# Down projection of a diffusion step: block sums of the activations formed in the gated unit, sums of the gate weights kept in scratch

## The chip, the cores and the metric

The kernel runs on one core of one Trainium2 chip. The metric is the device time of one launch in microseconds (us). PE is TensorE (PEld its weight loads), DVE VectorE, ACT ScalarE, POOL GpSimd and SP SyncE, on whose queue all transfers between DRAM and SBUF are issued, in order.

## The reference

One layer of a hybrid diffusion model is applied to 256 context tokens and 2048 latent tokens of 1024 features, in float32: modulated norm, an input projection, a gated DeltaNet scan beside a chunked mixer, an output projection with residual. Then comes the part that the change touches, the feed-forward block with D_FF = 2816, and a final norm:

```python
def swiglu(h, w_gate, w_up, w_down):
    return (jax.nn.silu(h @ w_gate) * (h @ w_up)) @ w_down

    h = rmsnorm(x, norm2_g) * (1 + sc2) + sh2
    x = x + g2 * swiglu(h, w_gate, w_up, w_down)
```

## The kernel before

The kernel is generated by a Python program with a small model of the engines (Model, line 44). Side work is written as generators, which a list of tasks (spawn, tick) inserts between matmuls at times that this model gives; a store is held in a list and issued (flush) when the model thinks that its source is ready, or when its source's buffer is to be reused. So the program's order on every engine follows from the model. lighter(n) picks VectorE or GpSimd for an elementwise operation by the model. The helper at line 149 issues every operation, so all rows of the profile carry that line and are told apart by their tiles.

Every matmul of the feed-forward block is split in three, since its operands are held as a rounded high part and a low part (split_to: a cast on ScalarE, then a subtraction on VectorE): high x high, low x high, high x low.

**The gated unit.** The 18 tiles of 128 tokens are handled in three groups (gi) of six, paired as three pairs. Within a group a loop runs over 22 column blocks f of w_gate and w_up (128 columns each), one unit each. Gate and up weights of one block, each cut into two halves of the 1024 rows, form a 2 x 2 block matrix (a11, a12 from w_gate, a21, a22 from w_up), and two token tiles form the other (b11, b12, b21, b22). Their product is formed with seven block products instead of eight (Winograd's form of Strassen's scheme), j = 0 to 6, with these left blocks:

- a11; s2 = s1 - a11; s3 = a11 - a21; a12; s1 = a21 + a22; a22; s4 = a12 - s2

One product j is 12 matmuls of 128 x 384 into one of six PSUM banks (pm), so a unit is 84. After each product, one or two additions on VectorE gather the results (tiles s, u, up); silu runs on ScalarE. The two results of a unit, gate times up for the first and for the second tile of each pair, go to DRAM scratch (fa_d, named a).

Loading and splitting of weights: w_load(i) loads both weight blocks of unit i (two of 512 KB) into tiles fraw, two units ahead. w_prep(i, j) forms the sums s1 to s4 (four per unit, in all 66 units, on VectorE or GpSimd) and splits block j of unit i into the tile wu, one unit ahead of its use. The right blocks of a group lie in seven tiles hb0 to hb6 (h2). For the groups 1 and 2 they are made while the group before runs (stage_next: normalise, transpose, split into tiles hu, store to scratch fh_d, named hbd), and loaded when the last unit of that group has used the tile (hb<-hbd). The last unit of group 0 or 1 isn't begun until stage_next has been issued completely.

In group 2 down_sums reads w_down (tiles dx), forms the four weight sums of the second block product (tiles do) and stores them (fw_d, named wt). The last unit of group 2 isn't begun until it has been issued completely.

**The down projection.** Now the activations are the left matrix, with two token tiles and two halves of D_FF (11 blocks f each) as blocks 11, 12, 21, 22, and w_down with its halves the right one. The nine pairs are handled in two runs of five and four. A run has seven products q, and in each a slot for every pair: 63 slots of 33 matmuls of 128 x 512 (11 blocks k, three parts). The product of slot s needs one left block of 704 KB, split into the tile ah. a_load(s) loads what it is made of into four buffers ar: three blocks for q = 0, two for q = 1, 2 and 5, one for q = 3, 4 and 6. a_prep(s) forms the sum of q = 1, 2 and 5 on VectorE (s1 for later slots is formed at q = 0, and s1 and s2 are stored in scratch fs_d, named sp), and splits. At the start of slot s, a_prep(s + 1) and a_load(s + 2) are issued. Right blocks are loaded into ur and split into un, one product ahead (u_load, u_step). From q = 3 on, every slot completes a quarter of two tiles' output (piece: times the gate g2b, on VectorE or GpSimd, plus the residual, square sum on ScalarE); finish normalises a tile's row block and stores it.

second_first prepares the first slots during the last unit of group 2.

Of the kernel before, what the change touches and what calls it, by code (L numbers as in the profile page):

```python
# [16 lines left out]
KB = 8  # L17
# [143 lines left out]
def hybrid_step(  # L161
# [375 lines left out]
    with tc.manual_schedule():  # L537
# [1233 lines left out]
        NW = 10  # L1771
        order_a = []
        groups = [[], [], []]
        fst = {}
        fa_d = [[dram.tile([P, HN, NFF, P], F32, name=f"a{gi}{i}") for i in range(2)] for gi in range(3)]
        fh_d = [[dram.tile([P, 2, 4, HN, P], F32, name=f"hbd{gi}{j}") for j in range(7)] for gi in range(3)]
        fw_d = [dram.tile([P, 4, 512], F32, name=f"wt{k}") for k in range(HF)]
        fs_d = [[dram.tile([P, HF, P], F32, name=f"sp{i}{p}") for p in range(NT // 2)] for i in range(2)]

        def f_open():  # L1780
# [7 lines left out]
            w_load(0)  # L1788
            spawn(w_first())

        def w_first():
            yield list(wraw[0])
            for j in range(7):
                w_prep(0, j)
                yield ()
            w_load(1)
# [5 lines left out]
        wraw, wtmp, wu = {}, {}, {}  # L1802

        def w_load(i):
            if i < 3 * NFF:
                f = i % NFF
                wraw[i] = [W.tile([P, KB, P], F32, tag="hh" if i > 1 else "fraw", name="fraw", bufs=NB if i > 1 else 2)
                           for _ in range(2)]
                for r, w in zip(wraw[i], (w_gate, w_up)):
                    nc.sync.dma_start(r, w[:, f * P:(f + 1) * P].rearrange("(k p) c -> p k c", p=P))  # L1810

        def w_prep(i, j):

            if i >= 3 * NFF:
                return
            F1 = fst["F1"]
            rg, ru = wraw[i]
            a11, a12, a21, a22 = rg[:, 0:4], rg[:, 4:8], ru[:, 0:4], ru[:, 4:8]
            if j == 0:
                wtmp[i] = [F1.tile([P, 4, P], F32, tag="wt", name=f"ws{n}", bufs=3) for n in (1, 2)]  # L1820
                lighter(512).tensor_add(wtmp[i][0], a21, a22)
            s1, s2 = wtmp[i]
            if j == 1:
                lighter(512).tensor_sub(s2, s1, a11)
            elif j == 2:
                lighter(512).tensor_sub(a21, a11, a21)
            elif j == 6:
                lighter(512).tensor_sub(s2, a12, s2)
            x = (a11, s2, a21, a12, s1, a22, s2)[j]
            u = F1.tile([P, 2, 4, P], F32R, tag="wu", name="wu", bufs=NW)  # L1830
            split_to(u[:, 0], u[:, 1], x)
            wu[i, j] = u
            if j == 6:
                del wraw[i], wtmp[i]
# [479 lines left out]
```

## Time and profile before

| | us |
|---|---|
| three runs | 3299.15, 3297.8, 3293.04 (median 3297.8) |
| profiled execution | 3295.81 |
| its span | 3294.1 |
| first and last matmul start of the gated unit | 1610.7 and 2667.6 |
| first and last matmul start of the down projection | 2698.9 and 3284.0 |
| busy in the span: PE, DVE, ACT, POOL | 2985.2, 2248.0, 1377.8, 699.9 |
| mean granted TensorE clock | 0.955 |

The profile gives, for one execution, busy times and waits. In a row of the timeline stand start, duration, engine, operation, out<-in by the names of tiles, shape and count, and in brackets the idle time before it with what ended it (the releaser). Rows of a tile give smallest, median and largest duration in ns, then first and last start. Rows of waits give who waited, for what, the sum in us, how often and the longest. In windows, a row is one stretch of the span in us from its start. Matmuls overlap, so their durations are longer than their pace. DMA share is the mean busy share of the core's 16 DMA engines.

### The profile page before, as it was taken

What the parts mean: (1) busy time and instruction counts of PE and PEld (TensorE: products, weight loads), DVE (VectorE), ACT (ScalarE), POOL (GpSimd) and SP (SyncE); (2) the same over time, 40 slices, a digit from 0 to 9 for tenths busy, and PEclk for the clock granted to TensorE, in tenths of its full rate; (3) what the DMA queues carried; (4) which work ended last, traced back from release to release, by engine and by line L of the source; (5) the groups of instructions that cost most, each with busy time, mean ns of one, the idle gap of its engine ahead of it and who ended that gap; (6) DMA issues with size and microseconds to landing.
All of it is one profiled execution on the core that took longest, in us unless ns stands there. A gap on an engine that the chain in (4) does not pass through costs nothing. (4 is left out here: it accounts for less than half of the span.)

```text
span 3294.1 us, 44868 instructions
## 1 busy us (share of the span) xinstructions
PE 2985.2 (91%) x15355; PEld 2580.0 (78%) x15355; DVE 2248.0 (68%) x3959; ACT 1377.8 (42%) x3124; POOL 699.9 (21%) x754
## 2 busy tenths in 40 slices
PE   8998998989999988998799999999999957999798
PEld 3776877768777777986699899999899945777586
DVE  3778676675875863655777777877788853676476
ACT  4765545455566421342443333333333322334233
POOL 1142312213222322232122221222012210011001
PEclk9999999999999989999899999999999978999899
DMA  7896977758678867985245556554755468777865
GB/s 234 285 267 174 301 213 220 227 159 266 197 220 262 231 218 243 323 280 194 83 117 146 143 169 199 146 146 133 246 158 150 131 215 298 243 235 258 292 228 196
DMA packets 762436, 695.59 MB, mean 211 GB/s; under 512 B 84922, under 2 KB 651583, under 8 KB 760161
## 3 DMA queue, kind: packets, MB, share of 16 engines
q1 hardware_dynamic: 762209, 692.72, 67.8%
q8 instruction: 123, 2.02, 0.3%
q14 instruction: 104, 0.85, 0.1%
HBM read 513.51 MB, written 179.10 MB: 210 GB/s over the span
## 5 line engine op out<-in xcount | busy, mean ns | idle before, releaser
L149 PE MATMUL pm<-hb,wu 128*128 128x384 f32 x5544 | 1004.5, 342 | 51.2 <-DVE u L149 20.2
L149 PEld LDWEIGHTS pm<-hb,wu 128*128 128x128 f32 x5544 | 985.5, 190 | 63.2 <-issue 32.7
L149 PE MATMUL pm<-un,ah 128*128 128x512 f32 x2079 | 513.0, 407 | 103.5 <-ACT ah L149 69.2
L149 PEld LDWEIGHTS pm<-un,ah 128*128 128x128 f32 x2079 | 404.8, 196 | 211.7 <-ACT ah L149 77.5
L149 PE MATMUL pd<-hT,wraw 128*128 128x384 f32 (+2 forms) x1152 | 431.8, 502 | 14.3 <-ACT rb L149 7.0
L149 PE MATMUL pd<-hT,whi 128*128 128x384 f32 (+2 forms) x1152 | 383.9, 383 | 0.0
L149 PEld LDWEIGHTS pd<-hT,wraw 128*128 128x128 f32 x1152 | 211.1, 195 | 110.5 <-ACT rb L149 7.9
L149 DVE TENSOR_TENSOR wu<-fraw,wu 128x512 fp32r<-128x512 f32 x264 | 217.5, 824 | 85.7 <-ACT wu L149 85.7
L149 PEld LDWEIGHTS pd<-hT,whi 128*128 128x128 f32 x1152 | 218.5, 194 | 16.9 <-issue 2.9
L149 ACT CAST wu<-fraw 128x512 fp32r<-128x512 f32 x264 | 156.9, 615 | 148.5 <-DVE fraw L149 83.8
L149 POOL TENSOR_TENSOR ws<-fraw,ws 128x512 f32<-128x512 f32 x63 | 81.5, 1293 | 611.5 <-DVE wu L149 539.5
L149 PE MATMUL pd<-hT,wlo 128*128 128x384 f32 (+2 forms) x576 | 198.3, 344 | 7.9 <-DVE wlo L149 7.9
L149 DVE TENSOR_TENSOR wu<-ws,wu 128x512 fp32r<-128x512 f32 x198 | 136.8, 691 | 82.3 <-ACT wu L149 82.3
L149 ACT CAST ah<-ar 128x1408 fp32r<-128x1408 f32 x63 | 86.3, 1370 | 227.1 <-DVE ar L149 158.6
L149 DVE TENSOR_TENSOR ah<-ar,ah 128x1408 fp32r<-128x1408 f32 x63 | 106.2, 1686 | 82.9 <-ACT ah L149 82.6
L149 DVE TENSOR_TENSOR un<-ur,un 128x512 fp32r<-128x512 f32 x154 | 109.7, 739 | 70.2 <-ACT un L149 70.1
L149 POOL TENSOR_TENSOR wlo<-wraw,whi 128x512 fp32r<-128x512 f32 x60 | 103.9, 1735 | 226.1 <-ACT whi L149 152.6
L149 DVE TENSOR_TENSOR u<-u,pm 128x384 f32<-128x384 f32 x264 | 144.1, 546 | 10.8 <-PE pm L149 10.8
L149 ACT CAST wu<-ws 128x512 fp32r<-128x512 f32 x198 | 121.7, 615 | 62.2 <-DVE ws L149 61.3
L149 DVE SCALAR_TENSOR_TENSOR acc<-rb,colT,acc 128x384 f32<-128x384 f32 (+1 forms) x252 | 142.1, 591 | 5.6 <-POOL acc L149 5.6
L149 POOL TENSOR_TENSOR C<-C,g2b 128x512 f32<-128x512 f32 x24 | 44.2, 1842 | 446.0 <-DVE C L149 333.4
L149 ACT ACTIVATE u<-u 128x384 f32<-128x384 f32 x66 | 34.7, 526 | 243.1 <-DVE u L149 243.1
(304 smaller groups left out, 4985.9 us busy)
## 6 DMA issues: line engine op xcount, KB each, us to landing
wraw<-in_w_in_dram SPq DMA_DIRECT2D x144, 512.0 KB
ar<-a SPq DMA_DIRECT2D x81, 704.0 KB
fraw<-in_w_gate_dram SPq DMA_DIRECT2D x66, 512.0 KB
fraw<-in_w_up_dram SPq DMA_DIRECT2D x66, 512.0 KB
ur<-wt SPq DMA_DIRECT2D x88, 256.0 KB
hbd<-hu SPq DMA_DIRECT2D x42, 512.0 KB
hb<-hbd SPq DMA_DIRECT2D x14, 1536.0 KB
ar<-sp SPq DMA_DIRECT2D x27, 704.0 KB
```

Source lines behind the costliest of these rows:

```text
L149: fn(*a, **k)
```

## The change

- The units of a group run in the order FO: 0, 11, 1, 12, and so on, so that the two units whose results are blocks of the same pair of halves follow each other.
- Behind each unit its activation block sums are formed on VectorE: one after the first unit of such a pair (s3), three after the second (s1, s2, s4), one or two operations per following product, through late_ev. All seven left blocks of the down projection go to scratch, fa_d[gi][0 to 6].
- a_load loads the one finished block, four slots ahead; a_prep only splits. fs_d is gone.
- Weight sums of the gated unit: in group 0 s1 and s2 are formed on GpSimd, s3 and s4 on VectorE, and stored in scratch ws_d (four of 256 KB per unit). In groups 1 and 2 three blocks are loaded from the weights and four from ws_d, each of 256 KB, one at each product j, a unit ahead of their splitting, into a ring of twelve slots (w_slot) in the six former tiles hh.
- Result tiles have two rings, ev with five and au with six buffers, instead of one with nine; down_sums yields at two places per step, for 1000 and 3000 ns of the model, instead of four; piece multiplies always on VectorE.

The diff's core:

```diff
-        fa_d = [[dram.tile([P, HN, NFF, P], F32, name=f"a{gi}{i}") for i in range(2)] for gi in range(3)]
+        FO = [f + HF * i for f in range(HF) for i in range(2)]
+        fa_d = [[dram.tile([P, HN, HF, P], F32, name=f"fa{gi}{b}") for b in range(7)] for gi in range(3)]
+        ws_d = [dram.tile([P, 4, 512], F32, name=f"ws{f}") for f in range(NFF)]
-        fs_d = [[dram.tile([P, HF, P], F32, name=f"sp{i}{p}") for p in range(NT // 2)] for i in range(2)]
...
+        def w_load(i, j):
...
+            f = FO[i % NFF]
+            def ld(w, k0):
+                x = w_slot()
+                nc.sync.dma_start(x, w[k0 * P:(k0 + 4) * P, f * P:(f + 1) * P].rearrange("(k p) c -> p k c", p=P))
+                return x
+            b = wraw.setdefault(i, [None] * 7)
+            if i < NFF:
+                if j in (0, 2, 3, 5):
+                    b[j] = ld(w_gate if j in (0, 3) else w_up, 4 * (j in (3, 5)))
+                    b[6] = b[3]
+            elif j in (0, 3, 5):
+                b[j] = ld(w_up if j == 5 else w_gate, 4 * (j > 0))
+            else:
+                b[j] = w_slot()
+                nc.sync.dma_start(b[j], ws_d[f][:, {4: 0, 1: 1, 2: 2, 6: 3}[j]].rearrange("p (k c) -> p k c", c=P))
...
+                if j == 0:
...
+                    nc.gpsimd.tensor_add(b[4], b[2], b[5])
+                    nc.gpsimd.tensor_sub(b[1], b[4], b[0])
+                    for k, n in ((4, 0), (1, 1)):
+                        store(ws_d[f][:, n], b[k].rearrange("p k c -> p (k c)"))
+                elif j == 2:
+                    nc.vector.tensor_sub(b[2], b[0], b[2])
+                    store(ws_d[f][:, 2], b[2].rearrange("p k c -> p (k c)"))
+                elif j == 5:
+                    nc.vector.tensor_sub(b[6], b[3], b[1])
+                    store(ws_d[f][:, 3], b[6].rearrange("p k c -> p (k c)"))
...
                 nc.vector.tensor_sub(o1[:, 0], b22, b12)
-                yield ()
                 nc.vector.tensor_sub(o1[:, 1], b12, b11)
                 store(fw_d[k][:, 0:2], o1)
-                yield ()
+                yield 1000
                 nc.vector.tensor_sub(o2[:, 0], b22, o1[:, 1])
-                yield ()
                 nc.vector.tensor_sub(o2[:, 1], b21, o2[:, 0])
                 store(fw_d[k][:, 2:4], o2)
-                yield 2000
+                yield 3000
...
+                assert not missing.get(fa_d[gi][q].name, 0)
+                nc.sync.dma_start(araw[s % 4], fa_d[gi][q][:, p])
 
         def a_prep(s):
             if s < len(slots):
...
-                if q == 1:
-                    nc.vector.tensor_sub(x, x, xs[1])
-                    store(fs_d[1][pi], x)
-                elif q == 2:
-                    x = xs[1]
-                    nc.vector.tensor_sub(x, xs[0], x)
-                elif q == 5:
-                    nc.vector.tensor_sub(x, x, xs[1])
                 hl = ahl[s % 2]
-                split_to(hl[:, 0], hl[:, 1], x)
-                if q == 0:
-                    lighter(HF * P).tensor_add(xs[1], xs[1], xs[2])
-                    store(fs_d[0][pi], xs[1])
+                split_to(hl[:, 0], hl[:, 1], araw[s % 4])
...
-                    if j == (1 if i else 5):
-                        w_load(i + 2)
                     w_prep(i + 1, j)
+                    if i:
+                        w_load(i + 2, j)
...
-                    while late_ev:
+                    if late_ev:
                         late_ev.pop(0)()
...
-                        a_store(gi, 0, f, u3)
+                        a_store(gi, 6 if e % 2 else 0, f, u3)
...
+                        def one(gi=gi, f=f, e=e, g=u2, up=up):
                             nc.vector.tensor_mul(up, g, up)
+                            if e % 2:
+                                a_store(gi, 4, f, up)
+                        if e % 2:
+                            def two(gi=gi, f=f, up=up, a11=kept[0], a21=kept[1]):
+                                nc.vector.tensor_add(a21, a21, up)
+                                a_store(gi, 3, f, a21)
+                                flush(src=a11.name)
+                                nc.vector.tensor_sub(a11, a21, a11)
+                                a_store(gi, 1, f, a11)
+                            def three(gi=gi, f=f, a12=u3, s2=kept[0]):
+                                x = ev("s4")
+                                nc.vector.tensor_sub(x, a12, s2)
+                                a_store(gi, 5, f, x)
+                            late_ev += [one, two, three]
+                        else:
+                            def two(gi=gi, f=f, a11=u3, a21=up):
+                                x = ev("s3")
+                                nc.vector.tensor_sub(x, a11, a21)
+                                a_store(gi, 2, f, x)
+                            late_ev += [one, two]
+                            kept = (u3, up)
...
-            lighter(512).tensor_mul(acc[:, c], acc[:, c], g2b[:, cx(t), c])
+            nc.vector.tensor_mul(acc[:, c], acc[:, c], g2b[:, cx(t), c])
...
                     a_prep(s + 1)
-                    a_load(s + 2)
+                    a_load(s + 4)
```

More of the change, by code (lines that the diff above doesn't have):

```diff
@@ L1800, in split_to, with w_slot, w_first @@
             (eng or nc.vector).tensor_sub(lo, x, hi)
[L1802 to L1810, printed above, removed]
+        wraw, wu, wslots, wcount = {}, {}, [], [0]
+        def w_slot():
+            x = wslots[wcount[0] % 12]
+            wcount[0] += 1
+            flush(src=x.name)
+            return x
+        def w_first():
+            for i in range(2):
+                g, u = (W.tile([P, 2, 4, P], F32, tag="fraw", name="fraw", bufs=2) for _ in range(2))
+                for x, w in ((g, w_gate), (u, w_up)):
+                    nc.sync.dma_start(x.rearrange("p i k c -> p (i k) c"),
+                                      w[:, FO[i] * P:(FO[i] + 1) * P].rearrange("(k p) c -> p k c", p=P))
+                wraw[i] = [g[:, 0], None, u[:, 0], g[:, 1], None, u[:, 1], g[:, 1]]
+                if i == 0:
+                    yield [g, u]
+                    for j in range(7):
+                        w_prep(0, j)
+                        yield ()
+        def w_load(i, j):
+            if i >= 3 * NFF:
+                return
+            f = FO[i % NFF]
+            def ld(w, k0):
+                x = w_slot()
+                nc.sync.dma_start(x, w[k0 * P:(k0 + 4) * P, f * P:(f + 1) * P].rearrange("(k p) c -> p k c", p=P))
+                return x
+            b = wraw.setdefault(i, [None] * 7)
[6 more added lines that the diff above has]
+            else:
+                assert not missing.get(ws_d[f].name, 0)
+                b[j] = w_slot()
+                nc.sync.dma_start(b[j], ws_d[f][:, {4: 0, 1: 1, 2: 2, 6: 3}[j]].rearrange("p (k c) -> p k c", c=P))
         def w_prep(i, j):
@@ L1891, in stage_first @@
                 b11, b21, b12, b22 = b1[:, 0:4], b1[:, 4:8], b2[:, 0:4], b2[:, 4:8]
-                t3, t2, t4 = (F1.tile([P, 4, P], F32, tag="ev", name=f"t{i}", bufs=9) for i in (3, 2, 4))
+                t2, t3, t4 = (F1.tile([P, 4, P], F32, tag=tag, name=f"t{i}", bufs=NE[tag])
+                              for i, tag in ((2, "ev"), (3, "ev" if len(placed) < 2 else "au"), (4, "au")))
                 lighter(512).tensor_sub(t3, b22, b12)
@@ L1916, in stage_next @@
                 b11, b21, b12, b22 = b1[:, 0:4], b1[:, 4:8], b2[:, 0:4], b2[:, 4:8]
[L1917 removed]
+                t3 = fst["F1"].tile([P, 4, P], F32, tag="ev", name="t3", bufs=NE["ev"])
                 for j in (2, 0, 3, 4, 1, 6, 5):
@@ L2015, in hybrid_step @@
         NU = 21
-        unit, udraw, araw, ahl, loaded = {}, [], [], [], {}
-        acount = [0]
+        unit, udraw, araw, ahl = {}, [], [], []
         def tile_at(slot):
@@ L2096, in second_first @@
                     araw.extend([t[:, 0], t[:, 1]])
-                a_load(0)
+                for s in range(4):
+                    a_load(s)
             elif j == 3:
@@ L2109, in hybrid_step @@
         for gi in range(3):
-            for f in range(NFF):
-                i = gi * NFF + f
-                if f == 4 and gi < 2:
+            for e, f in enumerate(FO):
+                i = gi * NFF + e
+                if e == 4 and gi < 2:
                     if gi == 0:
@@ L2141, in hybrid_step @@
                         h_first(j + 2)
-                    if j == (1 if i else 5):
-                        w_load(i + 2)
                     w_prep(i + 1, j)
-                    if gi == 2 and f == NFF - 1:
+                    if i:
+                        w_load(i + 2, j)
+                    elif j == 5:
+                        for _ in range(NB):
+                            t = W.tile([P, 2, 4, P], F32, tag="hh", name="ws", bufs=NB)
+                            wslots += [t[:, 0], t[:, 1]]
+                        for k in range(7):
+                            w_load(2, k)
+                    if gi == 2 and e == NFF - 1:
                         second_first(j)
-                    while late_ev:
+                    if late_ev:
                         late_ev.pop(0)()
```

81 lines of the change are left out of this document (22 added, 59 removed).

## The prediction

> **What bounds the kernel now.** I read the page's slices first, then the windows of the feed-forward part, then the timeline of TensorE (PE) in the down projection, then the tile ar. The profiled execution took 3295.8 us (span 3294.1 us and 1.7 us around it), 2.0 us below the median of 3297.8 us.
>
> ```profile
> span 3294.1 us, 44868 instructions
> PE   8998998989999988998799999999999957999798
> ```
>
> PE is full almost everywhere; the hole is in slices 33 and 34, and the slices behind it are thinner. Windows, with the columns us, busy time of PE, PEld, DVE (VectorE), ACT (ScalarE), POOL (GpSimd), granted clock, DMA share and GB/s:
>
> ```profile
> 1650.00:1944.00 294.00, 282.84 (x1600) 279.99 (x1599) 230.99 (x372) 116.48 (x228) 76.28 (x54) 0.99 0.50 137
> 2000.00:2316.00 316.00, 304.00 (x1715) 300.01 (x1714) 249.51 (x402) 120.59 (x238) 73.13 (x52) 0.99 0.50 136
> 2400.00:2500.00 100.00, 100.00 (x571) 100.00 (x570) 80.84 (x130) 35.11 (x68) 18.44 (x13) 1.00 0.50 145
> 2668.00:2699.00 31.00, 0.12 (x1) 0.12 (x1) 10.69 (x18) 3.83 (x5) 0.00 (x0) 0.57 0.77 276
> 2699.00:3284.00 585.00, 512.48 (x2078) 404.63 (x2079) 355.17 (x426) 199.39 (x311) 65.39 (x30) 0.94 0.74 254
> 2837.00:2934.00 97.00, 97.00 (x426) 79.80 (x426) 68.18 (x83) 37.78 (x58) 10.41 (x7) 1.00 0.66 215
> ```
>
> The first three lie in the gated unit's three token groups, where PE works without long holes, in the third without any wait in the window shown. Then PE stands still for 31 us. The down projection takes 585 us, with one stretch (last row) in which PE never waits. The timeline of PE shows that stretch and what the rest looks like (start, duration, count, idle time before and its releaser):
>
> ```profile
> 2776.80 25.38 PE L149 MATMUL pm<-un,ah 128*128 128x512 f32 x99 [0.87 <-DVE ah L149]
> 2836.78 97.91 PE L149 MATMUL pm<-un,ah 128*128 128x512 f32 x428 [0.73 <-DVE ah L149]
> 2936.07 0.50 PE L149 MATMUL pm<-un,ah 128*128 128x512 f32 x1 [1.39 <-ACT ah L149]
> 2977.86 52.44 PE L149 MATMUL pm<-un,ah 128*128 128x512 f32 x229 [1.16 <-DVE ah L149]
> ```
>
> Every stop lies at the start of a slot of 33 matmuls, where the split activation block ah isn't ready. The 428 matmuls without a stop are 13 slots, the last three of product 2 and all of products 3 and 4; products 3 and 4 load one block as it is and form no sum. Why ah is late stands at the tile ar and its neighbours:
>
> ```profile
> L149 PE MATMUL pm<-un,ah x2079: 387/389/796, 2698.9 to 3284.0; 128*128 128x512 f32 x189
> L149 SPq DMA_DIRECT2D ar<-a x81: 319/424/1915, 2690.6 to 3252.6; - x81
> L149 SPq DMA_DIRECT2D ar<-sp x27: 319/424/497, 2761.6 to 3232.2; - x27
> L149 SPq DMA_DIRECT2D sp<-ar x18: 319/320/773, 2704.3 to 3108.4; - x18
> L149 DVE TENSOR_TENSOR ar<-ar,ar x17: 1618/1626/2771, 2764.0 to 3022.2; 128x1408 f32<-128x1408 f32 x17
> L149 DVE TENSOR_TENSOR ar<-ar x12: 1617/1625/1627, 3069.2 to 3241.6; 128x1408 f32<-128x1408 f32 x12
> ACT ah L149 <- DVE ar L149: 158.6, 27, 15.0
> ```
>
> ScalarE's cast waits 158.6 us for VectorE's block sum, and that sum for loads: 108 loads and 18 stores of 704 KB for 63 slots, through four buffers, so a sum's second input is asked for only when the slot before it starts.
>
> **Down projection: -97 us.** The change drops the 29 VectorE sums and those on GpSimd, the 18 stores and 45 of the 108 loads, and loads each slot's block four slots ahead. SyncE's queue about four slots in, before (ar activations, sp kept sums, a activations in DRAM, ur raw weights):
>
> ```order
> L149 DMA ar_24323<-sp_10904 128x1408
> L149 DMA sp_10912<-ar_24324 128x1408
> L149 DMA ar_24324<-a_10865 128x1408
> L149 DMA ur<-wt_10893 128x512
> L149 DMA ur<-wt_10894 128x512
> L149 DMA ur<-wt_10895 128x512
> L149 DMA ar_24324<-sp_10905 128x1408
> L149 DMA sp_10913<-ar_24323 128x1408
> ```
>
> and after it (fa are the finished blocks):
>
> ```order
> L149 DMA ar_24550<-fa_10867 128x1408
> L149 DMA ur<-wt_10935 128x512
> L149 DMA ur<-wt_10936 128x512
> L149 DMA ar_24550<-fa_10867 128x1408
> L149 DMA ur<-wt_10937 128x512
> L149 DMA ur<-wt_10938 128x512
> L149 DMA ar_24549<-fa_10867 128x1408
> ```
>
> One load a slot is left, with no store between. At the undisturbed pace (97.91 us / 428 = 0.2288 us) 2079 matmuls take 475.7 us; they now take 585.1, so 109 us are lost. VectorE loses 47 us of sums (29 at 1.63) and gains the 24 gate multiplications that GpSimd did:
>
> ```profile
> L149 POOL TENSOR_TENSOR C<-C,g2b 128x512 f32<-128x512 f32 x24 | 44.2, 1842 | 446.0 <-DVE C L149 333.4 <-issue 112.5
> L149 DVE TENSOR_TENSOR C<-C,g2b 128x512 f32<-128x512 f32 x12 | 8.2, 685 | 0.0
> ```
>
> 24 x 0.685 = 16 us, so it goes from 355 to 324 us in a shorter stage, 66%. What stays late: the first slots, where four loads (2.8 MB, 10 us at 276 GB/s) stand ahead of the fifth weight block, about 4 us; and product 5 of the first run, where finished rows are normalised on VectorE. Four slots took 40 us there (from 2936.1 to just ahead of 2977.9; 132 x 0.2288 = 30 at full pace) although GpSimd helped; with a load and a sum a slot gone I keep 8 us for both runs' finishing slots. So -109 + 12 = -97; bounds -109 (nothing late) and -70 (a third of the loss is not the loads').
>
> **Hand-over to the down projection: -26 us.** Before, VectorE has the last weight sums of w_down (do) here:
>
> ```order
> L149 TENSOR_TENSOR do<-dx,do 128x512 x2
> L149 TENSOR_TENSOR do<-dx 128x512 x2
> L149 TENSOR_TENSOR do<-dx,do 128x512 x2
> L149 TENSOR_TENSOR do<-dx 128x512 x2
> L149 TENSOR_TENSOR do<-dx,do 128x512 x2
> L149 TENSOR_TENSOR up<-u_24148,up 128x384
> L149 TENSOR_TENSOR un<-ur,un 128x512 x2
> ```
>
> After, the same place reads
>
> ```order
> L149 TENSOR_TENSOR wu<-ws,wu 128x512
> L149 TENSOR_TENSOR u_24414<-u_24414,pm 128x384
> L149 TENSOR_TENSOR up<-u_24414,up 128x384
> L149 TENSOR_TENSOR un<-ur,un 128x512 x2
> L149 TENSOR_TENSOR s_24563<-u_24435,up 128x384
> ```
>
> since the sums end 10 units earlier. In the trace they fill the hole, each pair waiting for its load:
>
> ```profile
> 2666.36 1.29 DVE L149 TENSOR_TENSOR do<-dx 128x512 f32<-128x512 f32 x2 [6.32 <-DMA dx<-in_w_down_dram]
> 2684.50 1.29 DVE L149 TENSOR_TENSOR do<-dx 128x512 f32<-128x512 f32 x2 [6.42 <-DMA dx<-in_w_down_dram]
> 2698.88 0.80 PE L149 MATMUL pm<-un,ah 128*128 128x512 f32 x1 [30.99 <-ACT ah L149]
> ```
>
> What is late next is the first ah and un: asked for one step into a last unit of 14.7 us, against 8 us from the first ar load (2690.6) to the first matmul. I leave 5 us of 31; bounds -31 and -15.
>
> **Gated unit, first group: +15 us.** The gated unit's span and two kinds of operations in the first window (1650 to 1944):
>
> ```profile
> L149 PE MATMUL pm<-hb,wu x5544: 331/337/687, 1610.7 to 2667.6; 128*128 128x384 f32 x198
> L149 ACT CAST wu<-fraw 128x512 fp32r<-128x512 f32 x72 | 42.9, 616 | 27.4 <-DVE fraw L149 18.8 <-issue 8.7
> L149 DVE TENSOR_TENSOR wu<-ws,wu 128x512 fp32r<-128x512 f32 x54 | 37.1, 687 | 20.8 <-ACT wu L149 20.8
> ```
>
> It takes 1057 us. A unit is 84 matmuls, 100 us / 571 x 84 = 14.7 us when undisturbed (window 2400 to 2500). In the first window (18 units) VectorE is busy 231 of 294 us and PE is idle for 11. Weight sums and one activation product there:
>
> ```profile
> L149 DVE TENSOR_TENSOR fraw<-fraw 128x512 f32<-128x512 f32 x10 | 14.6, 1457 | 0.0
> L149 DVE TENSOR_TENSOR ws<-fraw 128x512 f32<-128x512 f32 x5 | 3.4, 685 | 0.0
> L149 DVE TENSOR_TENSOR ws<-ws,fraw 128x512 f32<-128x512 f32 x5 | 3.4, 686 | 0.0
> L149 DVE TENSOR_TENSOR up<-u,up 128x384 f32<-128x384 f32 x18 | 9.9, 552 | 0.0
> L149 POOL TENSOR_TENSOR ws<-fraw 128x512 f32<-128x512 f32 x14 | 23.8, 1703 | 11.5 <-DVE hu L149 7.6 <-DVE wu L149 4.0
> L149 POOL TENSOR_TENSOR ws<-ws,fraw 128x512 f32<-128x512 f32 x14 | 18.4, 1315 | 71.7 <-issue 63.4 <-ACT u L149 8.3
> ```
>
> Sums cost VectorE 21.4 us / 18 = 1.2 us a unit; now it has two (1.4 us) and, new, two activation block sums a unit (2 x 0.552). That is +1.3 us, 29 us over 22 units. What hides it is the 3.5 us a unit in which VectorE isn't busy, but most of that is waits for ScalarE, as the 20.8 us at wu show, and those come in its own order. Bounds 0 and +29; I take the middle.
>
> GpSimd goes from 54 operations in that window to two a unit, 36. A sum on VectorE beside GpSimd takes 1457 ns against 685. The Trainium skill (SBUF — State Buffer, "Who interferes with whom") says that a VectorE instruction with two SBUF inputs and a GpSimd one that reads SBUF exclude each other for the whole instruction. By that rule GpSimd's 76.28 us falls by a third, 25 us, which would pay for the 29; that is the first rival.
>
> **First group to second: +10 us.** The staging of group 1 (hu) is emitted later. On VectorE before, two units ahead of the last one:
>
> ```order
> L149 TENSOR_TENSOR t_17434<-hh 128x512
> L149 TENSOR_TENSOR hu<-t_17434,hu 128x512
> L149 TENSOR_TENSOR wu<-ws_17310,wu 128x512
> L149 TENSOR_TENSOR u_17339<-u_17339,pm 128x384
> L149 TENSOR_TENSOR hu<-hh,hu 128x512
> L149 TENSOR_TENSOR wu<-fraw,wu 128x512
> ```
>
> and after, in the last unit, as a block:
>
> ```order
> L149 TENSOR_TENSOR u_17761<-u_17761,pm 128x384
> L149 TENSOR_TENSOR t_17885<-hh 128x512
> L149 TENSOR_TENSOR hu<-t_17885,hu 128x512
> L149 TENSOR_TENSOR hu<-hh,hu 128x512 x2
> L149 TENSOR_TENSOR hh<-hh 128x512
> L149 TENSOR_TENSOR hu<-hh,hu 128x512
> ```
>
> Behind it wait the evictions (u<-u,pm), and the reload of hb, which reads what hu stored. Seven hu took 20 us in the trace, and the reload already cost PE 10.7:
>
> ```profile
> 1830.42 1.54 DVE L149 TENSOR_TENSOR t<-hh 128x512 f32<-128x512 f32 x1
> 1850.49 0.69 DVE L149 TENSOR_TENSOR hu<-hh,hu 128x512 fp32r<-128x512 f32 x1 [1.96 <-ACT hu L149]
> PE pm L149 <- DMA hb<-hbd: 10.7, 5, 4.9
> ```
>
> Six PSUM banks of 2.1 us each (14.7 / 7) let PE run 12.6 us ahead, so 20 - 12.6 = 7 are exposed, and the reload starts as much later; I take +10, bounds 0 and +25.
>
> **Groups 1 and 2: -9 us.** No weight sum is left there (7 of 7 blocks are loaded), so VectorE loses 1.2 us or more a unit and gets 1.1. GpSimd is silent. PE's waits for VectorE in 2000 to 2316,
>
> ```profile
> PE pm L149 <- DVE u L149: 9.7, 7, 2.7
> ```
>
> should mostly go: -9, bounds -12 and 0. Group 2 had none.
>
> **Transfers: 0.** In the gated unit:
>
> ```profile
> DMA packets 237114, 161.63 MB, mean 153 GB/s; under 512 B 5744, under 2 KB 229360, under 8 KB 235248
> q1 hardware_dynamic: 237040, 160.65, 51.7%
> ```
>
> The change adds 23 MB of stored weight sums, 35 MB of loads (seven blocks of 256 KB instead of four, in 44 units) and 19 MB of activation blocks (seven of 192 KB for two units instead of four): 239 MB. At 153 / 0.517 = 296 GB/s they would take 807 us of 1057, so they stay beside the matmuls; loads are asked for a unit ahead. Bounds 0 and +59 (239 MB at the span's mean of 211 GB/s is 1132 us). The last multiplication before the end is on VectorE instead of GpSimd: -1.
>
> Sum: -97 - 26 + 15 + 10 - 9 + 0 - 1 = -108, from 3295.8 to 3188; with the 2.0 us to the median, 3190 us.
>
> **The rivals.** *The first group costs nothing* (0.18): less GpSimd pays for the new VectorE work, 3190 - 15 = 3175. For it, the 1457 against 685 ns; against it, VectorE's waits for ScalarE, which stay.
>
> *The first group is held by its sums* (0.15): GpSimd's two sums wait for the unit's last load, and ScalarE's cast of the second waits for both. Issue 0.4 (the ar rows), landing 8.4, sums 1.7 + 1.3, cast and subtraction 0.6 + 0.7 make 13.1 us, under 14.7; the landing is the longest that the chain of waits showed for 704 KB,
>
> ```profile
> 2823.43 8.43 DMA ar<-a
> ```
>
> so it decides from about 10 us on. At 3 us too long in 20 units: 3250.
>
> *The down projection's stops are only in part the loads'* (0.08): 50 us stay instead of 12, 3228. Against it, products 3 and 4 ran clean with the same splits.
>
> *Slower* (0.04): the transfers become the bound of the gated unit. That decides when 239 MB get through at under 202 GB/s (1073 + 108 us); at 190 it ends at 3375. Against it, 254 GB/s in the down projection at a share of 0.74. That the change doesn't do what it says is excluded at the hole and in the queue by the orders above.
>
> **How the numbers follow.** The forecast has 0.55. Its range alone is 3165 to 3215; with the first two rivals, and the third, 3155 to 3252. A difference of 0.2% (7 us) is about what a measurement of this kernel can tell; only the last rival ends above, so faster 0.95, same 0.01, slower 0.04.
>
> **What would show it.** Right: 2079 matmuls in 475 to 500 us, no hole over 10 us ahead of them, ACT ah waiting for DMA or PE and never long; GpSimd silent after the first group. Wrong in its steps: PE waits for DVE u of over 40 us in the first group, a wait for hb over 30 us, or stops at ah that name DVE un or C. Wrong as a whole: PE waits in groups 1 and 2 released by loads of ws.

## The result and the profile after

The changed kernel takes 3186.5 us (median of four runs, 3184.8 to 3193.4) against 3298.5 us for the kernel before on the same chip: a ratio of 0.967, interval 0.965 to 0.9685. The forecast was 3190 us, in a range of 3155 to 3252. The profiled execution took 3193.4 us, 6.9 above the changed kernel's median, so what follows compares two executions that lie 3 us under and 7 us over their medians.

On the page after, the thin slices of PE behind slice 32 are gone, GpSimd (POOL) is silent from slice 26 on, and the thinnest slice of PE is now 26, where the first group ends:

```profile
span 3191.7 us, 45823 instructions
...
PE   8999999899989889899789889699999999999998
...
POOL 1143313223122322123312111000000000000000
```

The tile hb gives the span of the gated unit and what TensorE (PE and its weight loads) waited for in it:

```profile
L149 PE MATMUL pm<-hb,wu x5544: 331/337/689, 1612.9 to 2699.7; 128*128 128x384 f32 x198
...
  DVE u L149: 36.9, 25
  ACT s L149: 35.6, 4
  DMA hb<-hbd: 18.0, 11
```

The tile ah gives the span of the down projection:

```profile
L149 PE MATMUL pm<-un,ah x2079: 387/390/795, 2699.9 to 3182.5; 128*128 128x512 f32 x189
```

A token group is 5544 / 3 = 1848 matmuls; counted off in PE's timeline, they split the span, each group up to the end of its last matmul. The forecast's terms stand beside:

| stretch | before, us | after, us | difference | forecast |
|---|---|---|---|---|
| ahead of the gated unit | 1610.7 | 1612.9 | +2.2 | 0 |
| first group | 357.4 | 397.9 | +40.5 | +15 and +10 |
| second and third group | 362.3 + 337.4 | 351.7 + 337.5 | -10.5 | -9 |
| hole ahead of the down projection | 31.0 | 0 | -31.0 | -26 |
| down projection, first to last start | 585.1 | 482.6 | -102.5 | -97 |
| behind its last matmul's start | 10.1 | 9.2 | -0.9 | -1 |

The sum is -102.2, against spans of 3294.1 and 3191.7 (-102.4). The losses of the first group are larger than forecast, the gains of the rest as well. The forecast's terms add up to -108, so that the total came out near is in part luck: the first group's two terms cost 15.5 us more than forecast, and the later groups, the hole and the down projection gave 12.0 us more.

The windows show where PE is now full (columns: us, busy time of PE, PEld, DVE, ACT, POOL, granted clock, DMA share, GB/s). The rows are the first group, the 38 us behind its end, the second group, 100 us of the third, and the down projection:

```profile
1650.00:1944.00 294.00, 266.05 (x1465) 257.90 (x1464) 229.56 (x379) 103.41 (x198) 50.59 (x34) 0.96 0.63 190
...
2006.00:2044.00 38.00, 25.37 (x84) 22.55 (x84) 18.19 (x34) 9.30 (x18) 0.00 (x0) 0.68 0.99 374
2044.00:2316.00 272.00, 271.83 (x1561) 271.45 (x1562) 204.45 (x378) 111.08 (x222) 0.00 (x0) 1.00 0.76 223
2400.00:2500.00 100.00, 100.00 (x570) 100.00 (x570) 85.25 (x153) 34.22 (x68) 0.00 (x0) 1.00 0.97 325
...
2699.90:3183.00 483.10, 478.53 (x2080) 391.33 (x2079) 311.43 (x423) 198.40 (x311) 0.00 (x0) 0.99 0.64 212
```

The timeline of PE across the hand-over: the gated unit runs into the down projection without a hole, a few short stops follow in its first 14 us, and then 2045 of the 2079 matmuls run without one.

```profile
2679.66 20.40 PE L149 MATMUL pm<-hb,wu 128*128 128x384 f32 x115
2699.90 6.07 PE L149 MATMUL pm<-un,ah 128*128 128x512 f32 x26
...
2713.63 469.25 PE L149 MATMUL pm<-un,ah 128*128 128x512 f32 x2045 [1.86 <-DVE ah L149]
```

The end of the first group, on the same engine, is the worst place after the change. PE stops 15.5 us ahead of the group's last product and then waits at each product of the next unit for the reload of hb:

```profile
1980.37 10.77 PE L149 MATMUL pm<-hb,wu 128*128 128x384 f32 x60 [0.41 <-DVE u L149]
2006.60 4.21 PE L149 MATMUL pm<-hb,wu 128*128 128x384 f32 x12 [15.45 <-ACT s L149]
2014.76 4.18 PE L149 MATMUL pm<-hb,wu 128*128 128x384 f32 x12 [3.96 <-DMA hb<-hbd]
...
2044.16 54.94 PE L149 MATMUL pm<-hb,wu 128*128 128x384 f32 x309 [0.25 <-DMA hb<-hbd]
```

VectorE in these 20 us does nothing but the last staged blocks, one after another, and six of the seven hu wait for ScalarE:

```profile
1986.79 0.55 DVE L149 TENSOR_TENSOR u<-u,pm 128x384 f32<-128x384 f32 x1
1989.32 0.69 DVE L149 TENSOR_TENSOR t<-hh 128x512 f32<-128x512 f32 x1 [1.98 <-ACT hh L149]
...
1995.69 0.69 DVE L149 TENSOR_TENSOR hu<-hh,hu 128x512 fp32r<-128x512 f32 x1 [3.70 <-ACT hu L149]
...
2005.68 0.69 DVE L149 TENSOR_TENSOR hu<-hh,hu 128x512 fp32r<-128x512 f32 x1 [1.75 <-ACT hu L149]
2006.29 0.68 DVE L149 TENSOR_TENSOR wu<-ws,wu 128x512 fp32r<-128x512 f32 x1
```

and ScalarE waits for the store of the hu before last, since hu has two buffers. Its copy of PE's bank (s<-pm), for which PE stops, is queued behind that:

```profile
1995.04 0.62 ACT L149 CAST hu<-hh 128x512 fp32r<-128x512 f32 x1 [3.85 <-DMA hbd<-hu]
...
2005.03 0.62 ACT L149 CAST hu<-hh 128x512 fp32r<-128x512 f32 x1 [2.43 <-DMA hbd<-hu]
2005.55 0.61 ACT L149 CAST wu<-ws 128x512 fp32r<-128x512 f32 x1
2006.07 0.47 ACT L149 COPY s<-pm 128x384 f32<-128x384 f32 x1
```

### The profile page after: what moved, and what is told of

Its sections match the earlier page's. It is cut to its first block, busy times and chain, and to the rows that moved or that the text cites. A ratio compares the mean times of both kernels' runs of the same rounds, so it can differ in the third digit from the quotient of the medians.

```text
span 3191.7 us, 45823 instructions
## 1 busy us (share of the span) xinstructions
PE 2962.5 (93%) x15355; PEld 2575.4 (81%) x15355; DVE 2168.5 (68%) x4021; ACT 1375.9 (43%) x3124; POOL 483.3 (15%) x612
## 5 line engine op out<-in xcount | busy, mean ns | idle before, releaser
L149 PEld LDWEIGHTS pm<-hb,wu 128*128 128x128 f32 x5544 | 991.6, 192 | 87.0 <-issue 40.5
L149 PE MATMUL pm<-un,ah 128*128 128x512 f32 x2079 | 478.5, 392 | 4.4 <-DVE ah L149 1.9
L149 PEld LDWEIGHTS pm<-un,ah 128*128 128x128 f32 x2079 | 391.5, 188 | 91.2 <-DVE ah L149 2.4
L149 DVE TENSOR_TENSOR wu<-ws,wu 128x512 fp32r<-128x512 f32 x448 | 321.6, 718 | 168.1 <-ACT wu L149 168.1
L149 ACT CAST wu<-ws 128x512 fp32r<-128x512 f32 x448 | 257.2, 616 | 137.2 <-DVE ws L149 97.8
L149 ACT ACTIVATE s<-s 128x384 f32<-128x384 f32 x66 | 34.7, 525 | 240.5 <-DVE s L149 240.5
L149 DVE TENSOR_TENSOR un<-ur,un 128x512 fp32r<-128x512 f32 x154 | 101.6, 687 | 50.1 <-ACT un L149 47.4
L149 PEld LDWEIGHTS pd<-hT,wlo 128*128 128x128 f32 x576 | 112.3, 195 | 25.0 <-DVE wlo L149 10.0
L149 PE MATMUL po<-woa,yhi 128*128 128x512 f32 x288 | 107.8, 428 | 11.4 <-ACT yhi L149 9.9
L149 DVE TENSOR_TENSOR wlo<-wraw,whi 128x512 fp32r<-128x512 f32 x148 | 105.6, 727 | 10.2 <-ACT whi L149 9.9
```

What stands on the lines that cost most here:

```text
L149: fn(*a, **k)
```

## The experiments

Four questions were left: what makes the down projection fast (loads and sums gone, or the loads four slots ahead), what closed the hole, what the kept weight sums are worth, and what holds the first group. All stretches below are counted as in the table above, each from one profiled execution.

Two things limit what such a comparison shows. Ahead of the gated unit the changed kernel, after_again, two_ahead, old_pace, early and hu_three have the same instructions in the same order on PE, VectorE, ScalarE and GpSimd, and yet that stretch took from 1599.7 us (early) to 1612.9 us (changed); so a few us between whole times need not come from the edit, and the stretches are compared. And the generator places side work by its model, so an edit can move other work too: in hu_three and no_sums_first the second chain of hu also stands about half a unit earlier on VectorE, while in sums_on_vector VectorE's order in the first group is kept but for the moved sums and a few neighbours.

| kernel | ratio to before (interval) | first, second, third group, us | hole | down projection |
|---|---|---|---|---|
| changed | 0.967 (0.965 to 0.9685) | 397.9, 351.7, 337.5 | 0 | 482.6 |
| after_again | 0.9676 (0.9657 to 0.9694) | 397.6, 351.5, 335.9 | 0 | 482.6 |
| two_ahead | 0.9695 (0.9675 to 0.9715) | 394.5, 352.9, 335.9 | 0 | 485.4 |
| old_pace | 0.970 (0.968 to 0.9715) | 400.3, 353.2, 337.4 | 0 | 485.9 |
| before_new_pace | 0.995 (0.993 to 0.997) | 357.7, 364.7, 352.5 | 0 | 581.4 |
| sums_each_group | 0.995 (0.993 to 0.997) | 390.4, 399.8, 371.1 | 3.5 | 486.9 |
| early | 0.965 (0.963 to 0.966) | 394.2, 352.0, 336.8 | 0 | 482.9 |
| hu_three | 0.9615 (0.960 to 0.963) | 374.5, 352.1, 337.0 | 0 | 482.3 |
| before_three | 0.996 (0.995 to 0.9975) | 351.4, 359.6, 339.2 | 29.2 | 584.5 |
| no_sums_first | 0.960 (0.957 to 0.963) | 372.1, 354.3, 337.4 | 0 | 481.9 |
| sums_on_vector | 0.961 (0.958 to 0.964) | 375.4, 353.4, 335.3 | 0 | 482.2 |
| three_and_vector | 0.957 (0.955 to 0.959) | 364.8, 352.1, 336.5 | 0 | 482.6 |
| three_vector_early | 0.956 (0.954 to 0.958) | 359.8, 350.1, 337.4 | 0 | 482.1 |

**The loads' lead (two_ahead).**

```
-                for s in range(4):
+                for s in range(2):
                     a_load(s)
...
-                    a_load(s + 4)
+                    a_load(s + 2)
```

> The changed kernel with the down projection's activation blocks loaded two slots ahead instead of four (two loads at the start, then one at the start of each slot for the slot after next, as early as the kernel before asked for the second input of a sum). Nothing else differs. Theory (the loads, stores and sums that are gone are what counted): at most 15 us more, 3187 to 3201, down projection under 500 us. Rival (how far ahead a block is asked for is what counted): a load that lands after about 8 us is late by 1 to 2 us in most of the 63 slots of 7.6 us, 60 to 110 us more, 3246 to 3296, with ScalarE's cast to ah waiting for the loads to ar.

It came out at 3189.6 us. The down projection takes 485.4 us, 2.8 more, with stops of about 1 us at a few slots behind the first. Its timeline on PE, the two longest runs:

```profile
2713.57 249.00 PE L149 MATMUL pm<-un,ah 128*128 128x512 f32 x1089 [1.16 <-DVE ah L149]
...
2971.55 158.94 PE L149 MATMUL pm<-un,ah 128*128 128x512 f32 x693 [0.87 <-DVE ah L149]
```

A lead of two slots is enough once a slot needs one load and no sum. The gain is that of the loads, stores and sums that are gone; no run tells these three apart.

**The hole (old_pace and before_new_pace).** The first puts the old spacing of w_down's sums into the changed kernel, the second the new spacing into the kernel before.

```
                 nc.vector.tensor_sub(o1[:, 0], b22, b12)
+                yield ()
                 nc.vector.tensor_sub(o1[:, 1], b12, b11)
                 store(fw_d[k][:, 0:2], o1)
-                yield 1000
+                yield ()
...
-                yield 3000
+                yield 2000
```

> The changed kernel with the old spacing of w_down's weight sums in the third group (a pause after each of the four, 2000 at the end of a block, instead of two and two with 1000 and 3000); all else as changed. Theory (the hand-over's hole was made by where these sums stand, not by the activation block sums): the hole comes back, 26 to 31 us, so 3213 to 3218 us against 3186.5, and the down projection itself keeps its 476 to 485 us. Rival (the hole came from the load that the old down projection put on SyncE's queue and VectorE at its first slots, which is gone): within 3 us of 3186.5.

> The kernel before with one thing of the change: the spacing of w_down's weight sums (two and two, with 1000 and 3000). Its sums then end ten units before the last instead of standing, 14 of 44, in the last unit. Theory (the hole of 31 us is these 14 sums, each four waiting for their loads): 22 to 31 us less, ratio 0.991 to 0.993. Rival (the hole hides the activation loads and the first block sums, which are late next): 0 to 8 us less, ratio 0.9975 to 1.

Neither theory of old_pace was right as stated. PE goes from one stage to the other without a hole; the next kernel's hole is gone as well, but its third group has got stops that were not there before (PE's timeline of old_pace, then of before_new_pace):

```profile
2639.77 60.53 PE L149 MATMUL pm<-hb,wu 128*128 128x384 f32 x343
2700.14 3.33 PE L149 MATMUL pm<-un,ah 128*128 128x512 f32 x12
```

```profile
2438.69 15.38 PE L149 MATMUL pm<-hb,wu 128*128 128x384 f32 x84 [1.38 <-DVE u L149]
2455.45 15.10 PE L149 MATMUL pm<-hb,wu 128*128 128x384 f32 x84 [1.37 <-DVE u L149]
...
2659.77 19.29 PE L149 MATMUL pm<-hb,wu 128*128 128x384 f32 x109
2678.90 0.40 PE L149 MATMUL pm<-un,ah 128*128 128x512 f32 x1
```

In the order of VectorE's instructions 14 of the 44 sums stand in the last unit before, 3 in old_pace, none in the two kernels with the new spacing. So the hole needs the old spacing and something else that the change took away; the orders point to the gate's weight sums on VectorE, but no run leaves out these alone. Either the new spacing or the rest of the change closes it. But with the spacing alone the third group pays 15 us of the 31 back (337.4 to 352.5 us), since the sums now stand among evictions on a full VectorE: PE's stops end at 2539.6 us, behind the last of these sums at 2537.7. The kernel gains 0.5% where 0.7 to 0.9% was expected. In the changed kernel the third group takes 337.5 us, in old_pace 337.4, and the whole 31 us is gain.

**The kept weight sums (sums_each_group).** Every group loads four blocks a unit and sums again; the staging begins at the third unit of the first and of the second group. The run early (below) does the same in the first group alone, so it is what this one is compared with.

```
-            if i < NFF:
-                if j in (0, 2, 3, 5):
+            if True:
+                if j in (0, 2, 3, 5):
...
-            if i < NFF:
-                f = FO[i]
+            if True:
                 if j == 0:
...
-                    for k, n in ((4, 0), (1, 1)):
-                        store(ws_d[f][:, n], b[k].rearrange("p k c -> p (k c)"))
...
-                if e == 4 and gi < 2:
+                if e == 2 and gi < 2:
```

> The changed kernel without the kept weight sums: every group loads four weight blocks a unit and forms the four sums again (two on GpSimd, two on VectorE), nothing of them is stored; the staging of the second and of the third group begins at the third unit, as in the run named early for the second group. Theory (in the second group the reuse saves what VectorE gains, in the third nothing): against early (ratio 0.965) 8 to 15 us more, all of it in the second group, ratio 0.967 to 0.969. Rival one (the second and third group have room for the sums, and three loads a unit fewer shorten the reload of hb): ratio 0.962 to 0.966. Rival two (VectorE, now with activation sums too, is over its limit in all three groups): 30 us more or beyond, ratio 0.974 or above.

3275.1 us, 3% above early: the second rival. The profiled execution is the fastest of its runs, 3264.2 us, and its span is 88 us over that of early (3262.5 and 3174.7). The second group takes 399.8 us against 352.0, the third 371.1 against 336.8. The same 100 us of the third group, in early and then in sums_each_group:

```profile
2450.00:2550.00 100.00, 100.00 (x571) 100.00 (x570) 83.07 (x150) 34.31 (x67) 0.00 (x0) 1.00 0.94 303
```

```profile
2450.00:2550.00 100.00, 93.27 (x498) 89.03 (x497) 84.91 (x139) 31.59 (x60) 18.55 (x12) 0.97 0.70 228
```

and the subtraction to wu in this stretch of sums_each_group, 838 ns where it takes 687 in early:

```profile
L149 DVE TENSOR_TENSOR wu<-ws,wu 128x512 fp32r<-128x512 f32 x41 | 34.4, 838 | 14.5 <-ACT wu L149 14.5
```

Per unit of 84 matmuls VectorE is busy 84.91 / 498 x 84 = 14.3 us, where a unit takes 14.7 us at full pace; in early it is 12.2, with the sums of w_down in both. The activation sums are thus nearly free in the second and third group only with the weight sums gone from there. Whether VectorE's two weight sums a unit cost more, or GpSimd's two beside its instructions, this run doesn't separate. The first group forms its weight sums in both kernels and stores them only in early; it takes 390.4 us against 394.2, so these stores aren't what holds it.

**The block ahead of the last unit (early).**

```
-                if e == 4 and gi < 2:
+                if e == (2 if gi == 0 else 4) and gi < 2:
```

> The changed kernel with the staging of the second group begun at the third unit of the first group instead of the fifth, so that its last seven blocks hu stand among the evictions of the last two units and not as one block ahead of the last unit's. Theory (the 15.5 us stop of TensorE ahead of the last unit is that block): the stop goes, 10 to 16 us less, 3170 to 3177. Rival (VectorE has no room in the first group, so the same work stops TensorE elsewhere in it): within 4 us of 3186.5, with the waits for DVE u up by what the one stop loses.

The ratio falls to 0.965, 6 to 10 us under the changed kernel's two ratios; the first group of its profile takes 394.2 us, 3 to 4 less. The stop of 15.5 us is gone, but several of 1.9 to 2.8 us stand in its place, and the waits for DVE u in the group rise from 27 to 31 us (PE's timeline):

```profile
1966.75 3.91 PE L149 MATMUL pm<-hb,wu 128*128 128x384 f32 x12 [1.91 <-ACT s L149]
1972.83 3.50 PE L149 MATMUL pm<-hb,wu 128*128 128x384 f32 x12 [2.16 <-DVE u L149]
...
1996.71 3.43 PE L149 MATMUL pm<-hb,wu 128*128 128x384 f32 x12 [2.76 <-DVE up L149]
```

All stops of the group together fall from 52.1 to 41.6 us, but PE's busy time for the same matmuls rises from 348.8 to 355.6. By the trace this is the rival: moving the block moves most of the stop. The times leave up to 10 us of gain open, of which 3 to 4 us lie in the first group and most of the rest ahead of the gated unit, where the edit changes nothing.

**The staging's buffers (hu_three and before_three).** The second does the same to the kernel before.

```
-                    u = H.tile([P, 2, 4, P], F32R, tag="hu", name="hu", bufs=2)
+                    u = H.tile([P, 2, 4, P], F32R, tag="hu", name="hu", bufs=3)
...
-            x = Cp.tile([P, 512], F32, tag="x1", name="x1", bufs=4)
+            x = Cp.tile([P, 512], F32, tag="x1", name="x1", bufs=2)
```

> The changed kernel with three buffers instead of two for the staged blocks hu; to make room the residual's input x1 in the down projection has two buffers instead of four (expected to cost nothing: at most two are in use). Theory (ScalarE waits 21.5 us in the first group for the store of the hu before last, and holds everything behind it): TensorE's stops at the three hu chains of the first group, some 33 us together, fall by half, 10 to 20 us less, 3167 to 3177. Rival (the order on VectorE makes the stops, whatever the buffers): within 4 us of 3186.5.

> The kernel before with three hu buffers (and two for x1), nothing of the change. Theory (the two buffers became costly through the change, which left TensorE no lead in the first group): before, ScalarE waits 15.8 us there for stores of hu as well, but TensorE stops only 11.4 us for VectorE, so 0 to 8 us less, ratio 0.9975 to 1. Rival (the buffers cost both kernels alike, and the change only shows it): 12 to 25 us less, over the first and second group, ratio 0.992 to 0.996.

hu_three gains 0.5 to 0.6%, the upper end of the theory; its first group takes 374.5 us, 23 less, and its down projection is unharmed at 482.3. ScalarE's waits for the stores between 1650 and 1944 us, in the changed kernel and in hu_three:

```profile
ACT hu L149 <- DMA hbd<-hu: 11.6, 5, 4.5
```

```profile
ACT hu L149 <- DMA hbd<-hu: 0.6, 2, 0.3
```

before_three lies between its two theories: its first group gains 6.0 us and its second 2.7. So the two buffers cost before something too, and four times as much after the change.

**VectorE's load in the first group (no_sums_first and sums_on_vector).** The first leaves out the activation block sums of the first group (blocks are stored unsummed), the second moves the weight sums from GpSimd.

```
-                                nc.vector.tensor_add(a21, a21, up)
+                                if gi:
+                                    nc.vector.tensor_add(a21, a21, up)
```

and likewise for the other three sums;

```
-                    nc.gpsimd.tensor_add(b[4], b[2], b[5])
-                    nc.gpsimd.tensor_sub(b[1], b[4], b[0])
+                    nc.vector.tensor_add(b[4], b[2], b[5])
+                    nc.vector.tensor_sub(b[1], b[4], b[0])
```

> The changed kernel without the activation block sums of the first group: the two sums a unit on VectorE are left out there and unsummed blocks are stored in their place (same stores, same sizes), so the first group's outputs are of other data. Theory (VectorE is what stops TensorE in the first group; 44 sums of 0.55 us, 24 us, leave it): the stops that name DVE u between the hu chains go, 10 to 15 us off the gated unit's 1087 us, ratio to the kernel before 0.962 to 0.964 against 0.967. Rival (the chain of load, GpSimd's two sums, ScalarE's cast holds the first group): ratio 0.966 to 0.968, with ScalarE's wait for DVE ws and GpSimd's for loads as they were.

> The changed kernel with the two weight sums that GpSimd forms for each unit of the first group formed by VectorE instead (40 sums of 0.69 us, 27 us more VectorE work; GpSimd silent in the first group). Theory of the price lists (VectorE's work counts in full, as the +15 us of the forecast assumed): 10 to 25 us more, ratio 0.970 to 0.974. Rival (a GpSimd sum stretches the VectorE work beside it, as 799 ns against 687 for the subtraction to wu shows, some 23 us in the 294 us window, so moving it costs nothing or gains): ratio 0.964 to 0.968, and the subtraction to wu back at 687 ns in the first group.

Without the activation sums the first group takes 372.1 us, 26 less: more than the theory's 10 to 15, and the rival is out. With 40 more sums on VectorE it takes 375.4, 22 less: the theory of the price lists is wrong in sign. The groups of VectorE in the changed kernel between 1650 and 1944 us,

```profile
L149 DVE TENSOR_TENSOR wu<-ws,wu 128x512 fp32r<-128x512 f32 x116 | 92.6, 799 | 46.1 <-ACT wu L149 46.1
...
L149 DVE TENSOR_TENSOR ws<-ws 128x512 f32<-128x512 f32 x33 | 25.5, 774 | 0.0
```

that of GpSimd there,

```profile
L149 POOL TENSOR_TENSOR ws<-ws 128x512 f32<-128x512 f32 x34 | 51.4, 1511 | 251.2 <-DMA ws<-in_w_up_dram 143.1 <-DMA fa<-up 33.9 <-DMA fa<-s 20.8
```

and VectorE's in the same stretch of sums_on_vector, in which the subtraction to wu is back at 686 ns:

```profile
L149 DVE TENSOR_TENSOR wu<-ws,wu 128x512 fp32r<-128x512 f32 x125 | 85.8, 686 | 34.7 <-ACT wu L149 34.7
L149 DVE TENSOR_TENSOR ws<-ws 128x512 f32<-128x512 f32 x71 | 48.6, 685 | 0.6
```

The whole first group in windows: the kernel before, the changed kernel and sums_on_vector, each from the first matmul of the group to the end of its last:

```profile
1610.71:1968.06 357.35, 339.42 (x1897) 334.05 (x1898) 283.98 (x456) 145.38 (x282) 85.38 (x60) 0.98 0.47 131
```

```profile
1612.87:2010.80 397.93, 348.76 (x1896) 337.14 (x1896) 307.19 (x513) 147.27 (x282) 60.22 (x40) 0.94 0.61 184
```

```profile
1603.05:1978.40 375.35, 344.06 (x1896) 338.49 (x1896) 305.47 (x554) 148.44 (x282) 0.00 (x0) 0.95 0.65 196
```

VectorE is busy for 307.19 / 22 = 14.0 us a unit with GpSimd's help and for 305.47 / 22 = 13.9 us without it, with two sums more in nearly every unit. What GpSimd takes off VectorE, it adds again to the instructions beside it. The busy time stays the same, so it doesn't explain the 22 us. What fell are PE's waits for DVE u in the group (27.0 to 11.5 us) and VectorE's for ACT wu (58.9 to 39.8 us); why a VectorE that is as busy is late less often isn't shown.

**Together (after_again, three_and_vector, three_vector_early).** The edits are those above, combined.

> The changed kernel itself once more, as the reference for the two runs beside it on the same chip. Expected: ratio to the kernel before 0.965 to 0.968, first group 394 to 400 us by the matmul counts.

> The changed kernel with three hu buffers (and two for x1) and with the first group's two weight sums a unit on VectorE, both together; alone they took the ratio from 0.967 to 0.9615 and 0.961. Theory (two causes: stretched VectorE work between the hu chains, and the chains' waits for their stores): most of both adds up, 28 to 36 us less than the changed kernel, ratio 0.956 to 0.9585. Rival (both cure the same stops): 16 to 24 us less, ratio 0.960 to 0.962.

> As three_and_vector, and the staging of the second group begun at the third unit of the first group. With VectorE relieved, the theory expects that what early could not bring (4 us alone) now comes, since there is room for the last seven hu: 6 to 12 us less than three_and_vector, ratio 0.953 to 0.956. Rival: within 3 us of three_and_vector.

On one chip with the kernel before at 3290.9 us, the changed kernel takes 3188.3, three_and_vector 3148.4 and three_vector_early 3144.4 us. The two cures take 33 us off the first group together, where each alone takes 22 to 23: by this stretch less than their sum, as if they met in part at the same stops. By the times they add up: 40 us between the medians, 35 us by the ratios, against 35 to 41 us for the two ratios alone. The ratio is inside the theory's range; how far the cures overlap stays open. early adds 4 us, less than its theory's 6 to 12 and just over its rival's 3: not decided. three_vector_early beats both kernels, by 1.4% (3144.4 / 3188.3) and 4.4%. In its first group VectorE is as busy as in the changed kernel, and the group is 38 us shorter (its window from first matmul to last):

```profile
1598.98:1958.84 359.86, 341.44 (x1896) 335.95 (x1896) 305.96 (x555) 149.00 (x284) 0.00 (x0) 0.97 0.69 206
```

At its group switch PE runs through to the reload, and what is left there is the wait for hb:

```profile
1919.97 38.86 PE L149 MATMUL pm<-hb,wu 128*128 128x384 f32 x204 [3.48 <-ACT hu L149]
1962.88 3.63 PE L149 MATMUL pm<-hb,wu 128*128 128x384 f32 x12 [4.04 <-DMA hb<-hbd]
```

## Why the prediction was right, and where it was not

**Down projection, -97 forecast, -102.5 measured.** Right in mechanism: two_ahead shows that it is not the longer lead, which leaves the transfers and sums that are gone. The term kept 12 us over the undisturbed 475.7; 6.9 were needed (482.6), 5.9 of them in the first 13.7 us (34 matmuls, 7.8 us at full pace). The 8 us kept for the slots of product 5, where rows are finished, were not needed: there is no stop there.

**Hand-over, -26 forecast, -31.0 measured.** The hole is gone, and nothing was late next. The reason given, that the sums end earlier, was right, but it named one cause where there are two. before_new_pace shows that the new spacing closes the hole by itself, at 15 us in the third group; old_pace shows that the rest of the change closes it too, without the new spacing and at no cost to the third group (337.4 us).

**First group, +15 forecast.** Up to the stop at 1991.2 us the group lost 23.0 us against before (378.3 us for 1836 matmuls against 355.3). The size of the added work was about right: over the whole group VectorE's busy time rose from 283.98 to 307.19 us, 1.05 us a unit where 1.3 was counted. The step that was mis-sized took the middle of its bounds, 0 and +29, as if half of that work would hide; the loss up to the stop is as long as all of it (23.2 us). That the two lengths agree is no rule either, since what the work costs hangs on what stands beside it: with nearly the same VectorE work (305.96 us) three_vector_early takes 359.8 us instead of 397.9, and hu_three alone takes off nearly as much (23.4 us) as no_sums_first (25.8 us). So the loss came with the added work, but a third hu buffer, GpSimd's silence and the earlier staging take nearly all of it off again with the work in place. The kernel before would gain from the third buffer too: before_three takes 351.4 us, so 8.4 us lie between it and three_vector_early. How much of the loss belongs to which can't be said.

The GpSimd price that the forecast weighed as its first rival is real: with GpSimd silent the subtraction to wu takes 686 ns instead of 799. It hangs on the rule in the Trainium skill ("SBUF — State Buffer", "Who interferes with whom") that a VectorE instruction with two SBUF inputs and a reading GpSimd one exclude each other, and these numbers agree with it. But the rival drew the wrong end from it. GpSimd's work fell by a third, 76.28 to 50.59 us, as forecast, and that did not pay for the new sums; taking GpSimd out altogether took 22 us off, and left VectorE's busy time as it was.

**First to second group, +10 forecast, +17.5 measured** (40.5 less 23.0). The block of hu took about 20 us, as forecast from its rows. What failed is "Six PSUM banks of 2.1 us each (14.7 / 7) let PE run 12.6 us ahead, so 20 - 12.6 = 7 are exposed": at the block's start (1987.3 us, behind the eviction at 1986.79) PE had already used most of that lead, went on for 3.8 us and stopped for 15.5.

**Groups 1 and 2, -9 forecast, -10.5 measured.** Right, with more behind it than the sum saw: the second group also carries the slow running behind the first one's stop (84 matmuls busy for 25.4 us instead of 14.7 in the row from 2006 to 2044), and still gains. sums_each_group shows what the two halves are worth apart: 48 us and 34 us.

**Transfers, 0 forecast.** Right: 246.8 MB went through in the gated unit, where 239 were counted, and in the third group the DMA engines reach a share of 0.97 at 325 GB/s with no stop of PE. The rival that ended slower needed under 202 GB/s.

**The first group held by its sums.** Out: no wait of ScalarE or VectorE in the first group names POOL, hu_three leaves GpSimd's sums where they are and takes off 23 us, and PE's stops name DVE u and ACT s. The chance that the down projection stops for other reasons than loads is out as well.

## What to carry to other kernels

The time that added work costs is set by what waits around it, and neither its length nor the engine's busy share gives it alone. A unit takes 14.7 us at full pace. At 14.0 us of VectorE work a unit the changed kernel's first group had 52 us of PE's stops, at 13.9 us three_vector_early's had 22, and at 12.9 us that of the kernel before had 21. When a stage gets tighter, look for the small rings whose release is a store in it: a third buffer of 4 KB a partition was worth 23 us, nearly as much as leaving out 44 sums. And test edits that share an engine apart and together: the new spacing alone and the change without the kept weight sums each gave 0.5%, the whole change 3.3%. The kept weight sums alone were not run.

## What the runs showed of the hardware

- GpSimd's help saved VectorE nothing here: 40 sums of 1.5 us moved from GpSimd to VectorE left VectorE's busy time over the first group at 305.47 us against 307.19. Beside GpSimd's sums the subtraction to wu, with both inputs in SBUF, took 799 ns instead of 686; the addition u<-u,pm, with one input in PSUM, took 546 ns in both kernels.
- A stop costs more than its length. In the 38 us behind the 15.5 us stop, with further stops of up to 4.0 us, the granted clock was 0.68. The 12 matmuls at 2014.76 took 4.18 us at a granted clock of 0.50, those at 2028.78 took 2.35 us at 1.00. The Trainium skill ("TensorE: Matmul & The Clock Gate", "What's actually happening") puts the clock down to half after an idle window and up again after a busy one; the rows of 4.18 against 2.35 us fit that.
- A core's DMA engines at a share of 0.97 for 100 us, 325 GB/s, did not slow TensorE, VectorE or ScalarE: PE was busy for 100.00 of the 100 us with 570 matmuls (571 in the kernel before, at a share of 0.50), the subtraction to wu took 687 ns, as between 2044 and 2316 us at a share of 0.76, and ScalarE's cast to wu 615 ns against 614 in the kernel before.
